# The last 16 rows of a reciprocal row sum, op by op from one list

## The chip, the cores and the metric

One core of a Trainium2 chip. The metric is the device time of one execution in microseconds (us). The span of a profile, from the first to the last instruction, is shorter than the time of the same execution: 1.95 us in the middle for the kernel before. So spans and times are not mixed.

## The reference

```python
x = np.abs(np.random.randn(32, 512, 1024)).astype(np.float32) + 1e-6
return np.sum(1.0 / x, axis=-1).astype(np.float32)
```

There are 16384 rows of 1024 numbers, 67 MB. Each of the 128 partitions holds 128 consecutive rows; "row 112" below means that row of all partitions, 0.5 MB.

## The kernel before

The kernel divides nowhere. A row is cut in halves a and b, element by element: 1/a + 1/b = (a + b) / (a b). GpSimd makes the product p = a b (P). ScalarE turns it into r = 1/p with a logarithm (L) and an exponential (E), at half the row's elements. VectorE multiplies and sums (T) in one of two ways. For a *half-row sum* TensorE first makes a + b in PSUM (S, two matmuls with the identity), and VectorE sums (a + b) r over 512 elements. For a *whole-row sum* VectorE sums [a, b] times r over 1024 elements, which is the same up to the swap of halves that sums don't see. A few products are made on VectorE instead (V), with b first copied to PSUM by TensorE (B).

```python
A, B, C = (2, 0, 0), (2, 2, 0), (2, 2, 1)   # rows, half-row sums, products on VectorE
L, S1 = (1, 0, 0), (1, 1, 0)
LOADS = [[A, B, A, B], [A, B, A, C]] * 5 + [[A, B, A, C]]
LOADS += [[A, B], [A, C]] * 3 + [[A], [B], [A], [B], [A]]
LOADS += [[L, S1], [S1, S1], [L, S1]]
...
for (m, e, v), pr in zip(chunks, made):         # chunk by chunk
    ...
    nc.gpsimd.tensor_tensor(out=pr[:, v:, :], ...)               # P
    ...
    if waiting:
        sum_rows(*waiting)                                       # T of the chunk before
    keep(nc.scalar.activation(out=pr, in_=pr, func=Ln, scale=S)) # L
    ...
        keep(nc.scalar.activation(out=r, ..., func=Exp, scale=-1.0))  # E, right after it
```

Each ScalarE exponential directly follows the logarithm it depends on. And loads taper from 8 rows to 2; the last eight are of 2 rows.

Of the kernel before, what the change touches and what calls it, by code (L numbers as in the profile page):

```python
# [1 line left out]

# [6 lines left out]


@with_exitstack
def kernel(
    ctx: ExitStack,
    tc: tile.TileContext,
    x: bass.AP,
    out: bass.AP,
):










    nc = tc.nc
    f32 = mybir.dt.float32
    P = 128  # L30
    D = 1024
    H = D // 2
    F = 128

    R = 40

    S = float(2**17)



    A, B, C = (2, 0, 0), (2, 2, 0), (2, 2, 1)
    L, S1 = (1, 0, 0), (1, 1, 0)
    LOADS = [[A, B, A, B], [A, B, A, C]] * 5 + [[A, B, A, C]]
    LOADS += [[A, B], [A, C]] * 3 + [[A], [B], [A], [B], [A]]
    LOADS += [[L, S1], [S1, S1], [L, S1]]

    Ln = mybir.ActivationFunctionType.Ln
    Exp = mybir.ActivationFunctionType.Exp
    mult = mybir.AluOpType.mult
    plus = mybir.AluOpType.add  # L50

    x_v = x.flatten_outer_dims().rearrange("(p f) d -> p f d", p=P)
    out_v = out.flatten().rearrange("(p f) -> p f", p=P)

    act_sets = list(get_activation_tables(nc.m.arch).keys())
    nc.scalar.add_instruction(  # L56
        mybir.InstLoadActFuncSet(
            name=nc.get_next_instruction_name(),
            act_func_set_id=act_sets.index("natural_log_exp_and_others"),
            ins=[],  # L60
            outs=[],
        )
    )

    ppool = ctx.enter_context(tc.tile_pool(name="ppool", bufs=4))
    opool = ctx.enter_context(tc.tile_pool(name="opool", bufs=1))
    spool = ctx.enter_context(
        tc.tile_pool(name="spool", bufs=3, space=bass.MemoryType.PSUM)
    )
    bpool = ctx.enter_context(  # L70
        tc.tile_pool(name="bpool", bufs=1, space=bass.MemoryType.PSUM)
    )
    rpool = ctx.enter_context(
        tc.tile_pool(name="rpool", bufs=2, space=bass.MemoryType.PSUM)
    )

    ring = opool.tile([P, R, D], f32)
    sums = opool.tile([P, F], f32)
    ident = opool.tile([P, P], f32)
    make_identity(nc, ident)  # L80
    keep = tc.keep_in_program_order

    def add(bank, *halves):
        for k, half in enumerate(halves):
            i = nc.tensor.matmul(  # L85
                bank,
                lhsT=ident,
                rhs=half,
                start=k == 0,
                stop=k == len(halves) - 1,  # L90
            )
            keep(i)

    def sum_row(c, row, fac, out=None):
        i = nc.vector.tensor_tensor_reduce(  # L95
            out=row if out is None else out,
            in0=row,
            in1=fac,
            scale=S,
            scalar=0.0,  # L100
            op0=mult,
            op1=plus,
            accum_out=sums[:, c : c + 1],
        )
        keep(i)

    def sum_rows(c, xc, pr, sm, rc):
        m, e = xc.shape[1], len(sm)
        for j in range(e, m):
            row = xc[:, j, :].rearrange("p (h e) -> p h e", h=2)  # L110
            sum_row(
                c + j,
                row,
                rc[j - e].unsqueeze(1).to_broadcast([P, 2, H]),
                pr[:, e : e + 2, :] if j == e and e + 1 < m else None,
            )
        for j in reversed(range(e)):
            sum_row(c + j, pr[:, j, :], sm[j])

    waiting = None  # L120
    c0 = 0
    for chunks in LOADS:
        n = sum(m for m, _, _ in chunks)
        xt = ring[:, c0 % R : c0 % R + n, :]
        keep(nc.sync.dma_start(out=xt, in_=x_v[:, c0 : c0 + n, :]))  # L125

        made, q = [], 0
        for m, e, v in chunks:
            pr = ppool.tile([P, m, H], f32, tag="ps" if e else "pr")
            for j in range(v):  # L130
                b = bpool.tile([P, H], f32, tag="b")
                add(b, xt[:, q + j, H:])
                i = nc.vector.tensor_tensor(  # L133
                    out=pr[:, j, :], in0=xt[:, q + j, :H], in1=b, op=mult
                )
                keep(i)
            made.append(pr)
            q += m

        q = 0  # L140
        for (m, e, v), pr in zip(chunks, made):
            xc = xt[:, q : q + m, :]
            if v < m:
                i = nc.gpsimd.tensor_tensor(  # L144
                    out=pr[:, v:, :], in0=xc[:, v:, :H], in1=xc[:, v:, H:], op=mult
                )
                keep(i)
            sm = []
            for j in range(e):
                s = spool.tile([P, H], f32, tag="s")  # L150
                add(s, xc[:, j, :H], xc[:, j, H:])
                sm.append(s)
            if waiting:
                sum_rows(*waiting)
            keep(nc.scalar.activation(out=pr, in_=pr, func=Ln, scale=S))  # L155
            rc = []
            if e < m:
                r = rpool.tile([P, m - e, H], f32, tag="rc")
                keep(
                    nc.scalar.activation(out=r, in_=pr[:, e:, :], func=Exp, scale=-1.0)  # L160
                )
                rc = [r[:, l, :] for l in range(m - e)]
            if e:
                r = pr[:, :e, :]
                keep(nc.scalar.activation(out=r, in_=r, func=Exp, scale=-1.0))  # L165
            waiting = c0 + q, xc, pr, sm, rc
            q += m
        c0 += n
    assert c0 == F, c0
    sum_rows(*waiting)  # L170

    nc.sync.dma_start(out=out_v, in_=sums)


# [1 line left out]
_INS = ['x']  # L176
_OUTS = [((32, 512), 'float32')]


# [23 lines left out]
```

## Time and profile before

| | before |
|---|---|
| time, median of the first 3 runs | 171.06 us |
| span of the profile | 169.0 us |
| landing of rows 112-113 / of the last load | 143.59 / 160.93 us |
| end of GpSimd / ScalarE / VectorE | 163.91 / 165.77 / 166.53 us |
| issue of the store | 166.56 us |

The view below cuts the last 25 us into what the loads and what the engines set. It gives each engine's busy time (with its instructions) in the two stretches, then the granted clock, the share of the DMA engines and GB/s:

```profile
core 0: us, PE busy (x) PEld busy (x) DVE busy (x) ACT busy (x) POOL busy (x), PEclk, DMA share, GB/s
143.60:161.00 17.40, 15.15 (x34) 5.74 (x33) 15.34 (x36) 16.72 (x20) 17.40 (x11) 1.00 0.89 371
161.00:169.00 8.00, 3.27 (x8) 0.90 (x6) 4.95 (x14) 4.64 (x9) 2.90 (x3) 1.00 0.03 8
```

While the last 16 rows land, GpSimd is busy the whole time, ScalarE 96% and VectorE 88% of it. Afterwards the transfers are over and every engine still has 3 to 5 us of work. It is this work that the change rearranges.

### The profile page before, as it was taken

The page shows a single profiled execution, that of the slowest core. Times are in us where ns is not written, and L with a number is a line of the kernel's source. Part 1 is how long each engine was busy: PE and PEld are TensorE (multiplying, and loading weights), DVE is VectorE, ACT ScalarE, POOL GpSimd, SP SyncE. Part 2 cuts the span into 40 slices and gives each one's busy share as a digit, 9 for nine tenths or more (in the row PEclk, how much of TensorE's full clock was granted, in tenths as well). Part 3 has the DMA queues.
Part 4 walks back from the last instruction along what each step waited for, and adds up shares of the span by engine and source line. Part 5 has one row for each costly group of instructions (what it writes and reads, how often), then busy time and mean ns, then how long its engine had stood idle before and what let it go on. Part 6 is the DMA issues. An engine that isn't in the chain of part 4 may idle for free.

```text
span 169.0 us, 1265 instructions
## 1 busy us (share of the span) xinstructions
PE 130.5 (77%) x274; PEld 49.9 (30%) x274; DVE 121.1 (72%) x265; ACT 134.7 (80%) x135; POOL 140.7 (83%) x73
## 2 busy tenths in 40 slices
PE   0008899786988879875999869798879999997880
PEld 0003333331332233231343323243323433332320
DVE  0000777767987577776787689778789898988784
ACT  3002989978887988958979797898999999999992
POOL 1008999699995999679996998979999999999970
PEclk9999999999999999999699999999999999999999
DMA  6999999999999999999999999999999999999600
GB/s 217 411 457 403 457 411 457 411 457 411 457 405 442 426 442 423 442 421 442 419 450 419 442 426 428 395 426 428 426 434 426 426 415 419 417 426 421 256 0 16
DMA packets 3750, 67.24 MB, mean 398 GB/s; under 512 B 416, under 2 KB 544, under 8 KB 544
## 3 DMA queue, kind: packets, MB, share of 16 engines
q1 hardware_dynamic: 3744, 67.18, 93.3%
q8 instruction: 2, 0.03, 0.1%
q14 instruction: 4, 0.03, 0.0%
HBM read 67.11 MB, written 0.07 MB: 397 GB/s over the span
## 4 chain that ended last, share of the span: by engine, by line
DMA 52%; POOL 22%; ACT 13%; issue 8%; DVE 3%; POOLq 0%; DVEq 0%; SPq 0%
DMA ring<-in_x_dram 52%; POOL pr L144 22%; ACT pr L155 8%; ACT r L160 2%; ACT pr L165 2%; DVE ring L95 2%; DVE pr L95 1%; DVE pr L133 0%; DVE sums L95 0%; POOLq L144 0%; DVEq L198 0%; SPq L125 0%
## 5 line engine op out<-in xcount | busy, mean ns | idle before, releaser
L144 POOL TENSOR_TENSOR pr<-ring 128x1024 f32<-128x1024 f32 (+1 forms) x67 | 140.0, 2130 | 22.6 <-DMA ring<-in_x_dram 22.6
L85 PE MATMUL s<-ring,ident 128*128 128x512 f32 x256 | 122.9, 618 | 34.3 <-DVE sums L95 17.0
L155 ACT ACTIVATE pr<-pr 128x1024 f32<-128x1024 f32 (+1 forms) x67 | 67.9, 1013 | 28.2 <-POOL pr L144 28.2
L85 PEld LDWEIGHTS s<-ring,ident 128*128 128x128 f32 x256 | 46.6, 193 | 107.8 <-issue 60.1
L95 DVE CUSTOM_DVE_ANT_1 pr<-ring,r 128x1024 f32<-128x1024 f32 x31 | 37.9, 1221 | 44.2 <-ACT r L160 44.2
L95 DVE CUSTOM_DVE_ANT_0 pr<-pr,s 128x512 f32<-128x512 f32 x64 | 41.4, 683 | 0.0
L95 DVE CUSTOM_DVE_ANT_1 ring<-ring,r 128x1024 f32<-128x1024 f32 x33 | 40.1, 1217 | 0.6 <-issue 0.6
L165 ACT ACTIVATE pr<-pr 128x1024 f32<-128x1024 f32 (+1 forms) x34 | 34.2, 1007 | 1.1
L160 ACT ACTIVATE r<-pr 128x1024 f32<-128x1024 f32 (+1 forms) x33 | 33.1, 1002 | 1.0
L95 DVE DVE_READ_ACCUMULATOR2_ANT sums<- 128x1 f32 x128 | 10.5, 82 | 0.0
L85 PE MATMUL b<-ring,ident 128*128 128x512 f32 x18 | 10.0, 639 | 0.0
L133 DVE TENSOR_TENSOR pr<-ring,b 128x512 f32<-128x512 f32 x9 | 6.1, 683 | 0.7 <-PE b L85 0.7
L85 PEld LDWEIGHTS b<-ring,ident 128*128 128x128 f32 x18 | 3.4, 205 | 6.2 <-DMA ring<-in_x_dram 4.3
L56 ACT ACT_TABLE_LOAD x1 | 1.3, 1283 | 0.7 <-PEq L187 0.7
masks.py:197 POOL MEMSET ident<- 128x128 f32 x1 | 0.2, 205 | 0.3 <-POOLq L187 0.3
masks.py:199 POOL TENSOR_SCALAR_AFFINE_SELECT ident<-ident 128x128 f32<-128x128 f32 x1 | 0.3, 292 | 0.1
L187 POOL MEMSET const-float32-0.0<- 128x1 f32 x1 | 0.1, 98 | 0.2 <-issue 0.2
L187 POOL MEMSET const-bfloat16-1.0<- 128x1 bf16 x1 | 0.1, 101 | 0.0
L187 POOL MEMSET const-uint8-127<- 128x1 uint8 x1 | 0.1, 101 | 0.0
L187 POOL MEMSET const-float32-1.0<- 128x1 f32 x1 | 0.1, 99 | 0.0
## 6 DMA issues: line engine op xcount, KB each, us to landing
ring<-in_x_dram SPq DMA_DIRECT2D x11, 4096.0 KB, 37.7
ring<-in_x_dram SPq DMA_DIRECT2D x6, 2048.0 KB, 36.8
ring<-in_x_dram SPq DMA_DIRECT2D x8, 1024.0 KB, 28.2
out_dram<-sums SPq DMA_DIRECT2D x1, 64.0 KB, 1.5
```

Of the source, the lines that this page charges most:

```text
L56: nc.scalar.add_instruction(mybir.InstLoadActFuncSet(name=nc.get_next_instruction_name(), act_func_set_id=act_sets.index("natural_log_exp_ ...
L85: i = nc.tensor.matmul(bank, lhsT=ident, rhs=half, start=k == 0, stop=k == len(halves) - 1,)
L95: i = nc.vector.tensor_tensor_reduce(out=row if out is None else out, in0=row, in1=fac, scale=S, scalar=0.0, op0=mult, op1=plus, accum_out ...
L133: i = nc.vector.tensor_tensor(out=pr[:, j, :], in0=xt[:, q + j, :H], in1=b, op=mult)
L144: i = nc.gpsimd.tensor_tensor(out=pr[:, v:, :], in0=xc[:, v:, :H], in1=xc[:, v:, H:], op=mult)
L155: keep(nc.scalar.activation(out=pr, in_=pr, func=Ln, scale=S))
L160: nc.scalar.activation(out=r, in_=pr[:, e:, :], func=Exp, scale=-1.0)
L165: keep(nc.scalar.activation(out=r, in_=r, func=Exp, scale=-1.0))
L187: nc = _bacc.Bacc("TRN2", target_bir_lowering=False, num_devices=1)
```

## The change

The last 16 rows leave the loop and become a list of single operations. The letter is the operation, the number the row, "+" two rows at once. Each engine takes its own letters in the list's order. Cut from the diff ("..." marks the cuts, the last call is rewrapped):

```diff
-    L, S1 = (1, 0, 0), (1, 1, 0)
-    LOADS += [[A, B], [A, C]] * 3 + [[A], [B], [A], [B], [A]]
-    LOADS += [[L, S1], [S1, S1], [L, S1]]
+    LOADS += [[A, B], [A, C]] * 3
+    LAST = 112
+    LAST_LOADS = [2] * 6 + [1] * 4
+    ORDER = """
+        P112+ P114+ L112+ B117 E112+ P116 S115 V117 L114+ T113 L116+ P118 S118
+        T112 E114 E115 P119 T114 E116+ S119 P120 L118+ T115 D121 E118+ T117
+        L120+ S122 P122+ T116 E120+ T119 W124 T118 P125 L122+ T120 S123 P126
+        L125 T121 E122+ S126 P127 E125 T122 L126 T123 L127 S127 T125 E126 E127
+        T126 X124 T127
+    """
...
+        if kind == "P":
+            keep(nc.gpsimd.tensor_tensor(out=pr, in0=a, in1=b, op=mult))
+        elif kind == "D":
+            keep(nc.vector.tensor_tensor(out=pr, in0=a, in1=b, op=mult))
...
+        elif kind == "W":
+            keep(nc.scalar.activation(out=rows, in_=rows, func=Ln))
+        elif kind == "X":
+            keep(nc.scalar.activation(out=rows, in_=rows, func=Exp, scale=-1.0,
+                                      accum_out=sums[:, c : c + 1]))
```

Four ideas are in it. The order differs per engine, so that ScalarE can put another tile's work between a logarithm and its exponential. Products move from GpSimd to VectorE: V117, and D121, which reads both halves from SBUF (the prediction below says that the change's title counts three; the list has these two). Row 124 goes to ScalarE alone (W, X), which also sums it. And rows 124 to 127 are loaded one by one. Besides, rows 122 and 123 become one tile, and some rows change their kind of sum (seven half-row sums in place of eight).

More of the change, by code (lines that the diff above doesn't have):

```diff
@@ L168, with pair @@
         c0 += n
+    assert c0 == LAST, c0
+    c0 = LAST
+    for n in LAST_LOADS:
+        xt = ring[:, c0 % R : c0 % R + n, :]
+        keep(nc.sync.dma_start(out=xt, in_=x_v[:, c0 : c0 + n, :]))
+        c0 += n
     assert c0 == F, c0
     sum_rows(*waiting)
+    prs, rs, ss, bs = {}, {}, {}, {}
+    order = ORDER.split()
+    added = {int(op[1:]) for op in order if op[0] == "S"}
+    dead = set()
+    def pair(c):
+        k = (c - LAST) // 2
+        if k not in prs:
+            pr = ppool.tile([P, 2, H], f32, tag=("pr", "ps")[k % 2])
+            prs[k] = pr
+        return prs[k]
@@ new lines @@
+    for op in order:
+        kind, c, n = op[0], int(op[1:].rstrip("+")), 1 + op.endswith("+")
+        j = (c - LAST) % 2
+        rows = ring[:, c % R : c % R + n, :]
+        a, b = rows[:, :, :H], rows[:, :, H:]
+        pr = None if kind in "WX" else pair(c)[:, j : j + n, :]
+        if kind == "P":
+            keep(nc.gpsimd.tensor_tensor(out=pr, in0=a, in1=b, op=mult))
+        elif kind == "D":
+            keep(nc.vector.tensor_tensor(out=pr, in0=a, in1=b, op=mult))
+        elif kind == "B":
+            bb = bpool.tile([P, H], f32, tag="b")
+            add(bb, b[:, 0, :])
+            bs[c] = bb
+        elif kind == "V":
+            keep(
+                nc.vector.tensor_tensor(
+                    out=pr[:, 0, :], in0=a[:, 0, :], in1=bs[c], op=mult
+                )
+            )
+        elif kind == "S":
+            s = spool.tile([P, H], f32, tag="s")
+            add(s, a[:, 0, :], b[:, 0, :])
+            ss[c] = s
+        elif kind == "L":
+            keep(nc.scalar.activation(out=pr, in_=pr, func=Ln, scale=S))
+        elif kind == "E":
+            r = pr
+            if c not in added:
+                r = rpool.tile([P, n, H], f32, tag="rc")
+                rs.update({c + l: r[:, l, :] for l in range(n)})
+            keep(nc.scalar.activation(out=r, in_=pr, func=Exp, scale=-1.0))
+            if n == 2:
+                dead.add((c - LAST) // 2)
+        elif kind == "T" and c in added:
+            sum_row(c, pr[:, 0, :], ss[c])
+        elif kind == "T":
+            row = rows[:, 0, :].rearrange("p (h e) -> p h e", h=2)
+            k = (c - LAST) // 2
+            to = prs[k] if k in dead else None
+            dead.discard(k)
+            sum_row(c, row, rs[c].unsqueeze(1).to_broadcast([P, 2, H]), to)
+        elif kind == "W":
+            keep(nc.scalar.activation(out=rows, in_=rows, func=Ln))
+        elif kind == "X":
+            keep(
+                nc.scalar.activation(
+                    out=rows,
+                    in_=rows,
+                    func=Exp,
+                    scale=-1.0,
+                    accum_out=sums[:, c : c + 1],
+                )
+            )
```

## The prediction

> **What bounds the kernel now.** I read the page first: which row is full from end to end, and where it stops.
>
> ```profile
> span 169.0 us, 1265 instructions
> PE 130.5 (77%) x274; PEld 49.9 (30%) x274; DVE 121.1 (72%) x265; ACT 134.7 (80%) x135; POOL 140.7 (83%) x73
> ...
> DMA  6999999999999999999999999999999999999600
> ```
>
> No compute engine is above 83%, but the DMA row stands at 9 from slice 2 to slice 37. One slice is 169.0/40 = 4.2 us. So the 67 MB of input set the pace for some 160 us, and nothing in the diff moves fewer bytes. What the change can win lies after the last load. When that lands, the view of the last load's issue tells:
>
> ```profile
> L125 SPq DMA_DIRECT2D ring<-in_x_dram x1: 328/328/328, 141.2 to 141.2; - x1
> ...
> DMA to landing us min/median/max: 19.7/19.7/19.7
> ```
>
> Issued at 141.2, landed 19.7 us later: rows 126 and 127 are in at 160.9. The same view of the loads before it (issued 126.5, 131.4, 136.3; to landing 27.0, 24.6, 22.2) gives 153.5, 156.0 and 158.5: a pair of rows each 2.48 us. The span ends at 169.0, so the tail is 8.1 us. The chain of waits over that stretch and the timelines of ScalarE and VectorE show its content:
>
> ```profile
> 154.12 2.40 POOL pr L144
> 156.52 0.02 issue
> 156.54 1.06 ACT pr L155
> ...
> 162.23 0.53 ACT pr L155
> 162.76 0.02 issue
> 162.78 0.03 ACT pr L165
> 162.81 0.51 issue
> 163.32 0.62 ACT pr L155
> 163.94 0.02 issue
> 163.96 0.18 ACT r L160
> 164.14 0.56 issue
> 164.69 0.20 DVE ring L95
> ```
>
> ```profile
> 164.50 0.61 ACT L155 ACTIVATE pr<-pr 128x512 f32<-128x512 f32 x1
> 165.14 0.63 ACT L165 ACTIVATE pr<-pr 128x512 f32<-128x512 f32 x1
> ...
> 165.84 0.68 DVE L95 CUSTOM_DVE_ANT_0 pr<-pr,s 128x512 f32<-128x512 f32 x1
> 166.45 0.08 DVE L95 DVE_READ_ACCUMULATOR2_ANT sums<- 128x1 f32 x1
> 166.56 0.35 SPq L172 DMA_DIRECT2D out_dram<-sums  x1
> ```
>
> GpSimd's multiplies run with no gap to 163.9, but they are not on the chain after 156.5: ScalarE is. It works without a pause from 156.54 to 165.77, two to three operations behind GpSimd. Then follow one half-row sum on VectorE (165.84), the store at 166.56, and 2.4 us of store and finish that no edit touches. So the tail is bound by **ScalarE**, whose backlog is older than the last load: at 147.74 it begins the logarithm of rows 112-113, whose product GpSimd had finished at 147.2.
>
> **What the Trainium skill says.** (1) "ScalarE: Activation LUTs", section "What ACT_TABLE_LOAD costs": an ACTIVATE with immediates takes 186 ns + 0.833 ns per element, and back-to-back ones overlap by about 93 ns. The trace agrees: 1024 elements 1.04 us, 512 elements 0.61 us; start to start 0.96 and 0.53 where the next one does not need the one before (159.24 to 159.77), 1.07 and 0.65 where it does (158.59 to 159.24: logarithm, then exponential of the same tile). (2) "SBUF — State Buffer", section "Who interferes with whom": a VectorE instruction with two SBUF inputs contends with a GpSimd instruction that reads SBUF, and the later one waits for the whole of the other. No run here shows it yet: the VectorE product of before takes one operand from PSUM, where TensorE has copied it. (3) "DMA: Bandwidth & Descriptors", section "Measured (HBM→SBUF, 128 partitions, SWDGE, issued from GpSimd)", has the rule to batch loads to 1 MiB or more; the last four loads become 0.5 MB. The trace shows little of such a cost with queued loads: landings of 8, 4 and 2 rows lie 9.71, 4.89 and 2.48 us apart, so about 1.206 us per row plus 0.07 us per load.
>
> **The change part by part.** Rows 0 to 111 stay as they are. In the last 16:
>
> *Loads.* Rows 124 to 127 come one by one. From 156.0, with 1.206 + 0.07 = 1.275 each (estimate from the three distances): 157.3, 158.55, 159.85, 161.1. Two more loads cost 0.15 us on the last landing; row 124 and 126 come 1.2 and 1.1 us earlier.
>
> *GpSimd* loses three half-row products (117 and 121 to VectorE, though the title counts three there; 124 has none). A two-row multiply repeats each 2.33 us, a one-row one each 1.235. Before: 5 x 2.33 + 6 x 1.235 = 19.1 from 144.80, and the trace ends at 163.91. After: 3 x 2.33 + 7 x 1.235 = 15.6, so it could end at 160.4: it now waits for loads. By landings: P116 ends 150.75, P119 153.65, P120 154.9, P122-123 158.5, P125 159.95, P126 161.2, P127 161.2 + 1.29 = 162.5.
>
> *ScalarE*, the one that counts, keeps its start at 147.74. Its list has 13 instructions of 1024 elements (rows 124 in whole twice, against none before) and 8 of 512; before it had 10 and 12. By plain counts it loses: 3 x 0.96 more against 4 x 0.53 less is +0.76 us. But of 11 logarithm-exponential pairs only 3 still follow each other directly, so the 0.115 of dependence (1.07 less 0.96, 0.65 less 0.53) falls away 8 times, -0.92; and the waits for GpSimd of before, some 0.65 us (starts 1.24 apart instead of 0.96 at 154.21 and 156.54, and two small ones), shrink to 0.25, -0.4. Sum -0.56. Walking the list, start by start: L112 147.74, E112 148.81, L114 149.77, L116 150.79 (P116), E114 151.75, E115 152.28, E116 152.81, L118 153.77, E118 154.85, L120 155.81, E120 156.88, W124 157.84 (row landed 157.3), L122 158.80, L125 159.98 (waits 0.2 for P125), E122 160.51, E125 161.47, L126 162.00, L127 162.53 (P127 just done), E126 163.06, E127 163.59, X124 164.12, end 165.18. Before, the last ACTIVATE ended at 165.77: **0.6 us earlier**.
>
> *VectorE* does 8 whole rows (1.14 start to start), 7 half rows (0.61) and 2 products (0.61), 14.6 us in 149.4 to 165.2. Its order never makes the end wait: T112 must be done before E116 may write (152.66 against 152.81, the tightest hand-over), V117 needs TensorE's copy (148.55 + 1.1 = 149.7), D121 is wanted by L120 at 155.81. At the end: T122 161.6, T123 162.2, T125 162.8, T126 163.95, T127 164.56. Before, a whole row (1.14) and a half row came after the last-but-one exponential; now only half rows do. Store after T127: 164.56 + 0.72 (the distance 165.84 to 166.56) = 165.3. After X124, with some tenths for its accumulator: 165.18 + 0.15 = 165.35. Both end together, **1.2 us before the 166.56 of now**.
>
> Sum: 171.06 - 1.2 = 169.86 us; I put 169.9.
>
> **The rivals.** *GpSimd is the bound.* For it: its row is full to 163.9. Then 3 x 1.235 = 3.7 us would go and the time be 167.4. Against it: the chain leaves GpSimd at 156.5, and the last row lands at 161.1 in any case; its shortest way is 0.1 + 1.29 + 0.61 + 0.60 + 0.72 with hand-overs, a store at 164.5 and 169.0 us. That is the floor of any such reordering, 1.2% below now.
>
> *A new wait takes the gain.* D121 reads SBUF twice. By the second place of the skill it waits for P120 (153.6 to 154.9) and starts at 154.9 instead of 154.35, ends at 155.5 and still precedes L120 (155.81) by 0.3; GpSimd then idles until 156.1 anyway. If it is later, or T112 holds E116, ScalarE moves by as much: +0.3 to +0.7, so 170.2 to 170.6. The order is in-order on each engine, so one late release shifts all behind it. This is the rival I take most seriously.
>
> *The whole row costs ScalarE more than it saves elsewhere.* W124 and X124 are 2 x 0.96 against 1.18 for a normal row. If the accumulator needs a further step, X124 ends at 165.5 or later: 170.1 to 170.3. In favour: X124 is last in the list, the worst place. Against: T127 can only start at 164.56 whatever X124 does.
>
> *Small loads slow the stream.* 4 KB instead of 8 KB per partition; even doubled, the cost is 0.3 us at the last landing: 170.1.
>
> **Range and chances.** All rivals but the first add 0.2 to 0.7 and they don't all add; a mild gain beyond mine is capped by the floor of 169.0. So 169.4 to 170.6 should hold it 8 times in 10. Faster by 2% needs 167.64, below the floor: 0.01. Slower by 2% needs 174.5, 4.6 us of new waits in a tail of 8: 0.01. Within 2%: 0.98.
>
> **What would show it.** ScalarE without gaps over 0.25 us from 147.7 to about 165.2, its last instruction the exponential of row 124; GpSimd with gaps of 0.3 to 1.2 us before rows 118, 122 and 126, ending at 162.5; the last load landing at 161.1; the store near 165.4. D121 starting only when GpSimd's P120 ends shows the lock; starting at 154.35 denies it. I am wrong if ScalarE idles for more than half a microsecond before E116, L120 or L127 (a hand-over took the gain), if the last landing is after 161.5 (the loads), or if the store starts before 164.9 (then ScalarE was not the bound as I walk it).

## The result, and the profile after

| | before | after |
|---|---|---|
| time, median (6 runs each) | 171.12 us | 170.11 us |
| landing of rows 112-113 | 143.59 us | 143.84 us |
| landing of row 127 | 160.93 us | 161.32 us |
| end of GpSimd / ScalarE / VectorE | 163.91 / 165.77 / 166.53 us | 162.74 / 165.49 / 165.55 us |
| issue of the store | 166.56 us | 165.61 us |
| from the landing of rows 112-113 to the store | 22.97 us | 21.77 us |

The ratio is 0.994, 95% interval 0.9928 to 0.9953: 0.6%, within the 2% that count as the same. Ratios are the mean time of one kernel's runs over that of the other's of the same rounds, so not quite the ratio of the medians.

The table's last row is the measure that I use for all kernels below. A stream of loads shifts by some tenths between executions (rows 112-113 land anywhere from 143.6 to 144.5 in the profiles here), and the difference of these two moments of one trace takes that shift out.

The chain that ended last, of the profile after (start, length, what):

```profile
141.35 17.48 DMA ring<-in_x_dram
...
158.97 1.29 POOL pr L211
160.25 0.02 issue
160.27 0.03 ACT pr L229
160.30 0.51 issue
160.81 1.05 ACT pr L235
161.86 0.02 issue
161.88 0.50 DVE pr L108
```

Before, this stretch was one run of ScalarE. Now the chain comes down from a load, that of row 125 (issued at 141.35, landed at 158.83), through GpSimd's P125, L125 and E122 to VectorE's run of last sums. ScalarE's and VectorE's timelines at the end:

```profile
158.12 1.04 ACT L247 ACTIVATE ring<-ring 128x1024 f32<-128x1024 f32 x1
159.06 1.04 ACT L229 ACTIVATE pr<-pr 128x1024 f32<-128x1024 f32 x1
160.27 0.63 ACT L229 ACTIVATE pr<-pr 128x512 f32<-128x512 f32 x1 [0.17 <-POOL pr L211]
...
164.36 1.04 ACT L250 ACTIVATE ring<-ring 128x1024 f32<-128x1024 f32 x1
165.30 0.18 ACT L250 ACTIVATION_READ_ACCUMULATOR ring<-ring 128x1 f32 x1
```

```profile
154.66 1.09 DVE L213 TENSOR_TENSOR pr<-ring 128x512 f32<-128x512 f32 x1
...
161.88 0.69 DVE L108 CUSTOM_DVE_ANT_0 pr<-pr,s 128x512 f32<-128x512 f32 x1 [0.35 <-ACT pr L235]
...
164.85 0.68 DVE L108 CUSTOM_DVE_ANT_0 pr<-pr,s 128x512 f32<-128x512 f32 x1
165.46 0.08 DVE L108 DVE_READ_ACCUMULATOR2_ANT sums<- 128x1 f32 x1
```

L247 and L250 are W124 and X124. ScalarE's one marked wait is 0.17 us, before L125, and its last step, the accumulator's read, ends at 165.49. VectorE ends at 165.55. Before, 0.79 us lay between ScalarE's end and the store, since a sum on VectorE followed; now it is 0.12. Of the 1.20 us, 0.67 come from there, and 0.53 from ScalarE's earlier end (counted from the landing). GpSimd, full before, now has holes:

```profile
151.45 3.75 POOL L211 TENSOR_TENSOR pr<-ring 128x512 f32<-128x512 f32 x3 [0.53 <-DMA ring<-in_x_dram]
156.44 2.37 POOL L211 TENSOR_TENSOR pr<-ring 128x1024 f32<-128x1024 f32 x1 [1.24 <-DMA ring<-in_x_dram]
158.96 3.78 POOL L211 TENSOR_TENSOR pr<-ring 128x512 f32<-128x512 f32 x3 [0.16 <-DMA ring<-in_x_dram]
```

Each hole is a wait for a load. From row 118 on, GpSimd has caught up with the transfers.

### The profile page after: what moved, and what is told of

It reads as the page before. It is cut to its first block, busy times and chain, and to the rows that moved or that the text cites. A ratio compares the mean times of both kernels' runs of the same rounds, so it can differ in the third digit from the quotient of the medians.

```text
span 168.2 us, 1264 instructions
## 1 busy us (share of the span) xinstructions
PE 129.1 (77%) x272; PEld 49.3 (29%) x272; DVE 121.6 (72%) x265; ACT 134.7 (80%) x135; POOL 137.5 (82%) x72
## 4 chain that ended last, share of the span: by engine, by line
DMA 79%; POOL 8%; issue 4%; DVE 3%; ACT 3%; SPq 1%; POOLq 0%; DVEq 0%
DMA ring<-in_x_dram 79%; POOL pr L157 7%; DVE ring L108 2%; ACT pr L168 2%; DVE pr L108 1%; SPq L138 1%; POOL pr L211 1%; ACT r L173 1%; ACT pr L235 1%; DVE sums L108 0%; ACT pr L178 0%; POOLq L157 0%; DVEq L285 0%; POOLq L211 0%; ACT pr L229 0%
## 5 line engine op out<-in xcount | busy, mean ns | idle before, releaser
L98 PE MATMUL s<-ring,ident 128*128 128x512 f32 x252 | 120.7, 616 | 33.8 <-DVE sums L108 17.1
L157 POOL TENSOR_TENSOR pr<-ring 128x1024 f32<-128x1024 f32 (+1 forms) x56 | 121.0, 2197 | 22.7 <-DMA ring<-in_x_dram 22.7
L168 ACT ACTIVATE pr<-pr 128x1024 f32<-128x1024 f32 x56 | 59.0, 1053 | 28.0 <-POOL pr L157 27.9
L178 ACT ACTIVATE pr<-pr 128x1024 f32<-128x1024 f32 x28 | 29.6, 1057 | 0.9
L173 ACT ACTIVATE r<-pr 128x1024 f32<-128x1024 f32 x28 | 28.8, 1028 | 0.9
L211 POOL TENSOR_TENSOR pr<-ring 128x512 f32<-128x512 f32 (+1 forms) x10 | 15.8, 1603 | 1.9 <-DMA ring<-in_x_dram 1.9
L229 ACT ACTIVATE pr<-pr 128x1024 f32<-128x1024 f32 (+1 forms) x9 | 8.0, 901 | 0.2 <-POOL pr L211 0.2
L235 ACT ACTIVATE r<-pr 128x1024 f32<-128x1024 f32 (+1 forms) x5 | 4.2, 850 | 0.1
L235 ACT ACTIVATE pr<-pr 128x512 f32<-128x512 f32 (+1 forms) x5 | 3.8, 787 | 0.0
L98 PE MATMUL bb<-ring,ident 128*128 128x512 f32 x2 | 1.1, 644 | 1.5 <-DMA ring<-in_x_dram 1.5
L247 ACT ACTIVATE ring<-ring 128x1024 f32<-128x1024 f32 x1 | 1.0, 1040 | 0.0
L250 ACT ACTIVATE ring<-ring 128x1024 f32<-128x1024 f32 x1 | 1.0, 1039 | 0.0
```

Source lines behind the costliest of these rows:

```text
L98: i = nc.tensor.matmul(bank, lhsT=ident, rhs=half, start=k == 0, stop=k == len(halves) - 1,)
L157: i = nc.gpsimd.tensor_tensor(out=pr[:, v:, :], in0=xc[:, v:, :H], in1=xc[:, v:, H:], op=mult)
L173: nc.scalar.activation(out=r, in_=pr[:, e:, :], func=Exp, scale=-1.0)
L178: keep(nc.scalar.activation(out=r, in_=r, func=Exp, scale=-1.0))
L211: keep(nc.gpsimd.tensor_tensor(out=pr, in0=a, in1=b, op=mult))
L235: keep(nc.scalar.activation(out=r, in_=pr, func=Exp, scale=-1.0))
```

## The experiments

Theory A: after the change ScalarE and VectorE end together and GpSimd works at the loads' heels, so each part matters by how far its absence pushes the latest of the three, and the parts need each other. Rival B: the gain is ScalarE's, from the interleaved order, as the prediction's largest term had it. Rival C: the gain is GpSimd's relief, product by product. All kernels below were correct, except the one that is wrong. They ran in three sets, each with the kernel before timed again (its median in brackets): pair loads, row 124, row 121 and adjacent exponentials on chip 2 (171.14 us); order alone, loads alone, row 121 through PSUM and no X124 on chip 10 while it was noisy (171.24; this is the "noisy set"); row 117, the control, row 121 through PSUM again and E122 first on chip 10, quiet (171.13). The first two sets have no control of their own, so they are compared by the ratio to before and by the traces.

### Undoing one part at a time

**One-row loads undone.**

```diff
-    LAST_LOADS = [2] * 6 + [1] * 4
+    LAST_LOADS = [2] * 8
```

> The changed kernel with the last four rows loaded as two pairs again. Theory A (three engines and the last landings end together, so the one-row loads are needed): rows 124-125 land together at 158.8 and 126-127 at 161.2, so GpSimd's product of row 126 starts at 161.4 instead of 160.2, that of 127 ends at 163.9 instead of 162.7, and the store comes 1.0 to 1.1 us later than in the changed kernel: about the time of before. Rival (loads are hidden by ScalarE's backlog): the last landing comes 0.1 us earlier and the end moves by -0.1 to +0.2 us.

Measured: 171.14 us (before 171.14), ratio 1.0002 (0.999 to 1.0015). From landing to store 22.79 us, 1.02 more than in the changed kernel. ScalarE and GpSimd:

```profile
159.01 1.06 ACT L246 ACTIVATE ring<-ring 128x1024 f32<-128x1024 f32 x1 [0.65 <-DMA ring<-in_x_dram]
...
164.10 0.63 ACT L228 ACTIVATE pr<-pr 128x512 f32<-128x512 f32 x1 [0.58 <-POOL pr L210]
```

```profile
156.61 3.72 POOL L210 TENSOR_TENSOR pr<-ring 128x1024 f32<-128x1024 f32 x2 [1.23 <-DMA ring<-in_x_dram]
161.54 2.52 POOL L210 TENSOR_TENSOR pr<-ring 128x512 f32<-128x512 f32 x2 [1.21 <-ACT pr L228]
```

W124 waits 0.65 us for its row, and L127 waits 0.58 us for a product that ends 1.3 us later than in the changed kernel (1.1 us with the shift of the loads taken out). The view names ScalarE as the releaser of the second GpSimd wait, but that is a case of the last semaphore being guessed: the load of rows 126-127 landed at 161.38 in this trace, and GpSimd starts 0.16 us later, much the same delay as behind the landing of row 125 in the changed kernel (158.83 to 158.96). In time the whole gain is gone; from landing to store 0.18 us of it is left. Theory A holds.

**Row 124 as any other row**, with ScalarE's list rearranged so that this has its best chance:

```diff
-W124 T118 P125 ... L125 T121 E122+ ... T125 E126 E127 T126 X124 T127
+T118 P124 P125 ... E122+ P126 L124 E124 T121 L125 ... T123 S127 T124 E126 L127 T125 E127 T126 T127
```

> The changed kernel, but row 124 done as any other (product on GpSimd, logarithm and exponential of 512 elements, whole-row sum on VectorE), its ScalarE list reordered to suit. Theory A: one more 1.24 us product before row 127's, one more 1.14 us sum on VectorE, ScalarE 1 us lighter: store 0.7 to 0.9 us later than in the changed kernel. Rival (the whole row costs ScalarE more than it saves elsewhere): equal or up to 0.4 us earlier.

Measured: 170.93 us, ratio 0.9989 (0.9976 to 1.0001); landing to store 22.63 us, +0.86. From the landing, GpSimd ends 1.03 us later than in the changed kernel (at 163.59), ScalarE 0.23 (165.54) and VectorE 0.90 (166.27). The whole row costs ScalarE 2 us, but takes 1.24 us from GpSimd and 1.14 us from VectorE, and ScalarE had room for W124 at 158. Without it, ScalarE waits there for a product, that of rows 122-123:

```profile
158.67 1.06 ACT L229 ACTIVATE pr<-pr 128x1024 f32<-128x1024 f32 x1 [0.66 <-POOL pr L211]
```

The rival falls.

**Row 121's product back on GpSimd.**

```diff
-P120 ... D121
+P120+ ...
```

> The changed kernel, but row 121's product back on GpSimd, as a pair with row 120. Theory A: GpSimd has a hole of 1.24 us there (it waits for row 122), L120 moves from 156.08 to about 156.35 and the hole of ScalarE before L125 absorbs it: 0.0 us, within 0.1. Rival C (the gain is GpSimd's relief, each product given away is worth 1.24 us): up to 1.2 us later.

Measured: 170.01 us, ratio 0.9938 (0.9924 to 0.9952); landing to store 21.77 us, as in the changed kernel. GpSimd's run from 151.38 to 158.73 has no hole any more; L120 starts 0.2 us later, and the end does not move. This product on VectorE buys nothing; rival C, which gave it 1.2 us, falls for this row.

**Row 117's product back on GpSimd**, with E114 and E115 ahead of L116 to fill ScalarE's wait:

```diff
-B117 E112+ P116 S115 V117 L114+ T113 L116+ P118 S118 T112 E114 E115
+E112+ P116+ S115 L114+ T113 S118 T112 E114 E115 P118 L116+
```

> The changed kernel, but row 117's product back on GpSimd as a pair with row 116, and the exponentials of rows 114 and 115 put before the logarithm of rows 116-117. Theory A: GpSimd's P118 starts 0.6 us later (after its hole of 0.53 is used up), L118 moves from 154.04 to about 154.55, and part of it reaches the end: 0.2 to 0.4 us later than the control. Rival C (each product taken off GpSimd is worth its 1.24 us): 1.2 us later.

Measured: 170.65 us, ratio 0.997 (0.9958 to 0.9982), so +0.52 us against the control below; landing to store 22.06 us, +0.29. In time that is a miss, above the range; in the trace it is a hit. The difference lies outside the profile's span: the time exceeds the span by 2.16 to 2.25 us in all five runs of this kernel and by 1.91 to 2.03 in the control's. The spans, 168.4 against 168.1 us in the middle, agree with the trace. The edit also brings back two direct pairs on ScalarE (L114 with E114, L116 with E116), so the 0.29 us are not the product's alone. And the trace shows what was not foreseen. GpSimd's product of row 120, one instruction of 128x512:

```profile
L210 POOL TENSOR_TENSOR pr<-ring x1: 1742/1742/1742, 154.3 to 154.3; 128x512 f32<-128x512 f32 x1
```

It takes 1.74 us instead of 1.28: VectorE's D121, with its two SBUF operands, had started first, and GpSimd was held. In the changed kernel it is the other way round: D121 takes 1.09 us (its line above) because GpSimd's P120 came first. Rival C (1.2 us) falls, but unlike row 121's this product matters: L118 starts 0.36 us later (0.55 from the landing), after a wait of 0.34 us for GpSimd.

**The control**, the changed kernel again in the same set as row 117's run:

> The changed kernel itself, unaltered, as the control on this chip: 1.0 us (0.994) below before, as in its first timing.

Measured: 170.13 us, ratio 0.9938 (0.9925 to 0.9951); landing to store 21.77 us.

**The interleaving undone**, same work and loads:

```diff
-L114+ T113 L116+ ... E114 E115 ... L122+ ... L125 T121 E122+ ... E125 ... L126 ... L127 ... E126 E127
+L114+ T113 ... E114 E115 ... L116+ E116+ ... L122+ ... E122+ L125 ... E125 L126 ... E126 ... L127 ... E127
```

> The changed kernel with the same work and loads, but on ScalarE every exponential directly after the logarithm of its own tile (rows 124's two instructions stay apart). Theory A: the dependence of 0.11 us per pair comes back, but part of it falls into ScalarE's waits for GpSimd, and VectorE's last sums start earlier: 0.1 to 0.3 us later than the changed kernel. Rival B (the prediction's term: interleaving alone is worth 0.92 us on ScalarE): 0.7 to 0.9 us later.

Measured: 170.46 us, ratio 0.9963 (0.995 to 0.9975); landing to store 22.12 us, +0.35. A third of the gain, a little above theory A's range and far below rival B's. But rival B's 0.92 us was too much to expect of this edit: it brings back only six dependences (rows 114, 116, 122, 125, 126 and 127), 0.69 us at the prediction's 0.115 each (an estimate). From the landing ScalarE ends 0.45 us later. It then never waits for a product: what dependence costs it, it partly takes from the wait before L125.

### One part alone

**The order alone**, on the work and loads of before:

```diff
-L112+ E112+ ... L114+ ... E114+ ... L122 E122 ... L126 E126 L127 E127     (as before, chunk by chunk)
+L112+ ... E112+ L114+ ... L122 ... L123 E122 ... E123 L124 ... L125 E124 ... E125 L126 ... E126 L127 E127
```

> The work and the loads of the kernel before (all 16 products on GpSimd, no whole row on ScalarE, loads of two rows), but ScalarE's and VectorE's order interleaved over tiles as in the changed kernel. Theory A (the order alone cannot help while GpSimd's last product ends at 164.1): ScalarE's last ACTIVATE hardly moves, store 0.0 to 0.3 us earlier than before, so about 170.9. Rival B (the prediction's term: 0.92 us of dependence on ScalarE): 0.7 to 0.9 us earlier than before.

Measured in the noisy set (its runs of before reach from 170.88 to 172.22): 171.2 us, ratio 0.9985 (0.9958 to 1.0012); landing to store 22.74 us, 0.23 less than before. This list is less interleaved than the expectation says: on ScalarE only the exponentials of rows 122 to 125 are apart from their logarithms, the other seven rows or pairs run as before. At 0.115 us each, rival B's price for the four is 0.46 us (an estimate), a ratio of 0.9973, which the interval holds. So this run does not refute the price; it shows that this much order brings no gain in time that stands clear of the noise, and its trace shows a wait that takes part of it. L125, earlier now, waits for its product:

```profile
162.40 0.63 ACT L228 ACTIVATE pr<-pr 128x512 f32<-128x512 f32 x1 [0.19 <-POOL pr L210]
```

The order of the changed kernel in full, on the old work, was not tried.

**The one-row loads alone**, on the kernel before:

```diff
-    LOADS += [[L, S1], [S1, S1], [L, S1]]
+    LOADS += [[L, S1], [S1], [S1], [L], [S1]]
```

> The kernel before with nothing changed but the last four rows loaded one by one. Theory A (GpSimd is behind the loads there and takes rows 124 to 127 no sooner): 0.0 us, within 0.2 of before, though in the changed kernel undoing these loads cost 1.04. Rival (the loads carry the gain by themselves): 0.8 to 1.0 us earlier than before.

Measured in the noisy set: 171.69 us, ratio 1.0032 (0.9993 to 1.0071); landing to store 22.83 us, 0.14 less than before. No gain in time. GpSimd's line in the two shows why:

```profile
149.59 14.46 POOL L144 TENSOR_TENSOR pr<-ring 128x1024 f32<-128x1024 f32 x9
```

```profile
148.06 16.79 POOL L210 TENSOR_TENSOR pr<-ring 128x1024 f32<-128x1024 f32 x10
```

The first is the kernel with loads alone, the second with the order alone: one unbroken run of products to 164.05 and 164.85. With all products on GpSimd it is behind the loads, so a row that lands earlier lies waiting (row 127 landed at 161.32 in the first, and its product began at 162.73), and ScalarE's better order waits for products. The other two parts, the moved products and row 124, were not tried alone.

### What sets the end

**Row 121's second half through PSUM**, so that VectorE's product does not contend with GpSimd:

```diff
-S119 P120 L118+ T115 D121
+B121 S119 P120 L118+ T115 V121
```

> The changed kernel, but row 121's second half is copied to PSUM by TensorE first, so that VectorE's product has one SBUF operand. Lock theory: the product's record shrinks from 1.09 to about 0.68 us, since it no longer waits for GpSimd's product of row 120. Theory A for the time: 0.0 us, within 0.1, because ScalarE wants it at 156.08 only and VectorE has slack later. Rival (the lock costs its 0.4 us at the end): 0.3 to 0.4 us earlier.

Measured in the noisy set: 170.37 us, ratio 0.9948 (0.9915 to 0.998); landing to store 22.27 us, +0.5: a miss. The product's wait was for TensorE's copy, 1.27 us, and TensorE ran at a lowered clock just then:

```profile
150.00:154.00 4.00, 4.00 (x7) 1.69 (x6) 3.85 (x6) 3.61 (x5) 3.07 (x3) 0.57 1.01 420
```

0.57 is the granted clock, against 1.00 in the changed kernel in that stretch. So it was run again:

> The copy-to-PSUM variant of row 121's product once more, because its first profile fell on a stretch of lowered TensorE clock (0.57 from 150 to 154) that delayed the copy, and on a noisy chip. Lock theory: product's record 0.68 us; without the clock dip the copy is ready near 155. Theory A for the time: within 0.15 us of the control. Rival (the copy's queue on TensorE costs more than the lock it avoids): 0.3 to 0.5 us later than the control even at full clock.

Measured: 169.99 us, ratio 0.9936 (0.9924 to 0.9948); landing to store 21.83 us. The product on VectorE:

```profile
L219 DVE TENSOR_TENSOR pr<-ring,bb x1: 689/689/689, 155.3 to 155.3; 128x512 f32<-128x512 f32 x1
```

0.69 instead of 1.09 us, and no gain in time: with theory A, the contention was real and cost nothing at the end. The direct form has the merit that it does not hang on TensorE's queue and clock.

**E122 ahead of L125**, which lets VectorE's last run begin sooner:

```diff
-L125 T121 E122+ S126 P127
+T121 E122+ L125 S126 P127
```

> The changed kernel with the exponential of rows 122-123 ahead of the logarithm of row 125, so that VectorE's last run of sums can begin 0.35 us earlier. Theory A: the last exponential of row 124 on ScalarE still ends at 165.5, so 0.0 to 0.1 us earlier than the control. Rival (VectorE alone sets the end): 0.3 to 0.4 us earlier.

Measured: 170.11 us, ratio 0.9945 (0.9932 to 0.9959), the control 0.9938; landing to store 21.72 us, 0.05 less. VectorE ends 0.22 us before ScalarE now (165.17 against 165.39), and the store waits for ScalarE:

```profile
164.25 1.04 ACT L249 ACTIVATE ring<-ring 128x1024 f32<-128x1024 f32 x1
165.20 0.19 ACT L249 ACTIVATION_READ_ACCUMULATOR ring<-ring 128x1 f32 x1
```

**The same without X124**, wrong (W124's own sum is stored in its place):

> Wrong result on purpose (row 124's output is a sum of logarithms): the changed kernel with the last exponential of row 124 left out and the exponential of rows 122-123 put ahead of the logarithm of row 125, so that ScalarE ends 1.1 us earlier and VectorE's last run of sums begins 0.35 us earlier. Theory A (VectorE and ScalarE end within 0.05 of each other; VectorE's own floor is the run from T122 on): store 0.3 to 0.4 us earlier than in the changed kernel, not more. Rival (ScalarE alone sets the end): 0.9 to 1.1 us earlier.

Measured in the noisy set: 170.54 us, ratio 0.9955 (0.9916 to 0.9994), too wide to tell 0 from 0.4 us, though it excludes the rival's 1 us (0.988). Landing to store 21.52 us, 0.25 less than the changed kernel; theory A said 0.3 to 0.4. ScalarE ended at 164.75 and VectorE at 165.56, so without X124 VectorE is next, close behind. T126 waited 0.15 us for its exponential there, which the expectation had left out.

### All together

| kernel | ratio to before | landing of rows 112-113 to store |
|---|---|---|
| before | 1 | 22.97 us |
| changed (control) | 0.994 (0.9938) | 21.77 (21.77) us |
| changed, pair loads | 1.0002 | 22.79 us |
| changed, row 124 as any other | 0.9989 | 22.63 us |
| changed, exponentials adjacent | 0.9963 | 22.12 us |
| changed, row 117's product on GpSimd | 0.997 | 22.06 us |
| changed, row 121's product on GpSimd | 0.9938 | 21.77 us |
| before, order alone (rows 122 to 125) | 0.9985 (noisy) | 22.74 us |
| before, one-row loads alone | 1.0032 (noisy) | 22.83 us |

Undone one by one, the four parts that matter are worth 1.02 + 0.86 + 0.35 + 0.29 = 2.5 us in the last column, though together they bring 1.20. Done alone, part of the order brings 0.23 and the loads 0.14, and neither a gain in time beyond the noise. They form a chain of conditions, not a sum. No variant beat the changed kernel beyond noise.

## Why the prediction was right, point by point

*The time.* 169.9 was predicted, 170.11 measured; the range of 169.4 to 170.6 holds it, and "within 2%" with it. The predicted move of the store, 1.2 us, is what the traces show from landing to store (22.97 to 21.77); in time it is 1.0. Most of the difference lies behind the store: the "2.4 us of store and finish that no edit touches" grew from 2.48 to 2.62 us. That the way from landing to store is hit to a hundredth (21.76 us by the prediction's figures) is luck: three terms are each off by less than a tenth and cancel (landing to L125 16.39 against 16.43, L125 to X124's end 5.20 against 5.12, from there to the store 0.17 against 0.21).

*What bounds the kernel.* Its statement that loads set the pace up to 160.9 and that only the 8 us after it can be won stands. "The tail is bound by ScalarE" holds for the kernel before by its chain, but the reading behind it is wrong in two places. ScalarE has no backlog "older than the last load", since it waited for products twice before that load landed:

```profile
154.21 1.06 ACT L155 ACTIVATE pr<-pr 128x1024 f32<-128x1024 f32 x1 [0.21 <-POOL pr L144]
...
156.54 1.06 ACT L155 ACTIVATE pr<-pr 128x1024 f32<-128x1024 f32 x1 [0.19 <-POOL pr L144]
```

And it is not "two to three operations behind GpSimd": its logarithms of rows 122 and 127 start 0.85 and 0.59 us behind the end of their products, one operation. The lag shrinks because ScalarE takes 1.18 us a row there and GpSimd 1.23. So in the kernel before, a faster ScalarE alone could bring its last logarithm forward by 0.6 us at most (an estimate from these starts): GpSimd, off the chain, delivers each product only just ahead of it. The prediction came out right because its walk kept GpSimd's products and the landings beside ScalarE, which its sentence on the bound does not.

*The walk of ScalarE* is the step that carried the number. It gave 165.18 for the end of X124; the trace has 165.40, and the stream of loads was 0.25 us later in that execution. Its one wait of 0.2 us for P125 is there (0.17). For the accumulator it put 0.15 us. The read is a further step, as its rival feared: 0.18 us long, but it starts 0.09 us before X124's end and so adds 0.09; the store follows 0.12 us later.

*The walk of VectorE* gave T127 at 164.56; it came at 164.85, again with the shift. "Both end together" is the profile's 165.49 and 165.55, and the exchange of E122 and L125 confirms it: the second to end took over within 0.05 us.

*D121.* The prediction had it held until P120's end and done at 155.5; P120 ended at 155.20 and D121 at 155.75. It still precedes L120, and removing it or its contention moved nothing. But its sign for the lock was wrong: D121 was to start "only when GpSimd's P120 ends". Its record starts at 154.66, as soon as VectorE is free, and the wait lies inside it: 1.09 us long, to 0.55 us behind P120's end.

*The hand-over T112 to E116*, called the tightest, seems to have bound: E116 started at 153.08, just behind VectorE's accumulator read (152.99), 0.64 us behind E115 instead of 0.53. The rival of a new wait thus came true by a tenth, but it was not felt at the end: in the control E116 came 0.54 us behind E115, and landing to store was the same 21.77 us, because ScalarE waits for P125 afterwards in both (0.17 and 0.18 us).

*Where its account was off.* The sum for ScalarE, +0.76 - 0.92 - 0.4, is fair arithmetic of that engine's time, but reads as if the interleaving were the main gain. Of its eight dependences only six are the order's (0.69 us); the other two go because rows 122-123 are one tile and row 124 is done otherwise. Undone, the six cost 0.35 us at the store. And the one-row loads stand in it as a cost of 0.15 us with two rows coming earlier; the walk used those earlier rows (W124 at 157.84 needs row 124), without saying that nearly the whole gain hung on them, 1.02 of 1.20 us. The cost itself was 0.11 us: the last four rows took 161.32 - 156.28 = 5.04 us against 160.93 - 156.00 = 4.93.

*Its signs.* GpSimd's holes were to come before rows 118, 122 and 126: they came before 118, 122 and 125 (0.53, 1.24 and 0.16 us). The last landing was to be 161.1, the end of GpSimd 162.5 and the store near 165.4: they were 161.32, 162.74 and 165.61, all late by the shift of the loads.

*The rivals.* "GpSimd is the bound", which promised 3.7 us, fell: with the holes as shown, GpSimd waits for loads. As one bound among others it stands, since row 117's product and row 124's matter. "The whole row costs ScalarE more" fell by experiment, +0.86 us without it. "Small loads slow the stream" was a tenth of a microsecond.

## What to carry to other kernels

Near the end of a pipeline, walk every engine's list by start times from the trace, with the landings as the clock: a sum of busy times per engine does not show which part is needed. When several engines end within a tenth of each other, parts of a change can be worth little alone and nearly everything when taken away, so test both ways. Compare traces from a common event, such as the landing of one load, rather than from the start.

## What the Trainium skill lacked or had wrong

- "ScalarE: Activation LUTs" says that an ACTIVATE can give an accumulator output, but not what that costs. The trace has a separate instruction behind it, 0.18 us long, which overlaps it by 0.09 us and adds 0.09, here at the very end. Behind W124 in the run without X124 it cost the same: the next instruction started 1.04 instead of 0.95 us after W124.
- "SBUF — State Buffer", section "Who interferes with whom", is borne out in both directions: a VectorE product with two SBUF inputs took 1.09 us behind a GpSimd product (0.69 us with one input in PSUM; two SBUF inputs without a GpSimd product beside it were not measured), and a GpSimd product 1.74 us instead of 1.28 behind a VectorE one. It has no figure for what remains after the release; here VectorE needed 0.55 us more after GpSimd's end (155.20 to 155.75), and as much behind P119 with row 117's product on GpSimd (154.37 to 154.92).
- "DMA: Bandwidth & Descriptors", section "Measured (HBM→SBUF, 128 partitions, SWDGE, issued from GpSimd)", has 341 GB/s for transfers of 1 MB and the rule to batch to 1 MiB or more; its table has no row for 0.5 MB and none for loads queued behind each other. Issued from SyncE and queued, loads of 1.05 MB landed each 2.48 us here, 423 GB/s, and loads of 0.52 MB each 1.26 us, 416 GB/s. Cutting the last loads cost 0.11 us and was a condition of nearly the whole gain.
